# A decoder block's opening re-ordered: scale and norm in one VectorE step, shift added where the halves are split

## The chip, the cores and the metric

The kernel runs on one core of a Trainium2 chip. The metric is the device time of one execution in microseconds (us), the median of several. Five engines run their own instruction queues in order: TensorE (PE in the profile, with its weight loads as PEld), VectorE (DVE), ScalarE (ACT), GpSimd (POOL) and SyncE (SP, which here only issues transfers).

## The reference

One decoder block over 2048 tokens of width 1024, in float32. What matters here is its head:

```python
c_act = jax.nn.silu(c)
ada = (c_act @ w_ada[l] + b_ada[l])[:, None, :]
shift, scale, gate = jnp.split(ada, 3, axis=-1)
h = _rms(x, g_pre[l]) * (1.0 + scale) + shift     # _rms: x * rsqrt(mean(x*x)+eps) * g
proj = h @ w_in[l]                                # 1024 x 4864
q, k, v, z_a, u_b, v_b, z_b, g_logits = jnp.split(proj, SPLIT_IDX, axis=-1)
q = _rope(...); k = _rope(...)                    # cos and sin of positions * inv_freq
```

Sliding-window attention, a spatial gating unit, two gated projections and an output projection follow; the change leaves them alone.

## The kernel before, in words

**Products.** Every large matrix product is split 2 x 2 and made of seven products of sums of quarters (Winograd's form), numbered p = 0 to 6. Each quarter is split into a high part in the fp32r format and the low rest, and a product of two quarters is three TensorE passes over four tiles of 128 rows: 12 matmuls of 128x512 (`mm3`, lines 158 to 164). One product is a *slot*. A slot needs a weight pair W (high by a ScalarE cast, line 207; low by a VectorE subtraction through line 146) and an activation tile T of four row tiles (high by ScalarE, line 614; low by VectorE, line 146).

**Order.** Nothing is scheduled by a planner: each engine runs its instructions in the order in which the program emits them. `w_get` (195) is called before every slot and lets `want` (181) prepare the weights three slots ahead: fetch (SP), weight sums `s13`, `s2`, `s4` (234 to 262), cast, low part. `later(n, f)` hangs work on the slot n ahead, before its matmuls, after them ("post"), or between their halves ("mid").

**The first 1024 tokens** are the opening. Three column blocks of `w_in` share the activation tiles: slots 0 to 20 are p = 0 for blocks 0, 1 and 2, then p = 1 for them, and so on; their accumulators are banks X and W, Y and Z, and the tile s. The 1024 tokens come as two halves h of 512, x transposed in eight row tiles `xh[kt][h]`. p = 0 needs half 0 and rows 0 to 511; p = 1 needs the difference of the halves, so half 1's statistics; p = 2 and later need rows 512 to 1023 as well, so the second half of scale and shift.

**Ahead of slot 0**, in program order: transfers of half 0, of the first half of w_ada (4 MB), of three weight quarters, of half 1. Ten dummy products `warm` (418). Squares of half 0 (528: ScalarE squares, VectorE adds). `rstd` (538: sums over partitions on TensorE, a VectorE copy, two GpSimd steps) and `rstd_out` (548: spread over the partitions by TensorE, copied by ScalarE). `ada_row` (560): the product c @ w_ada, 32 matmul instructions for each half. `xn` (555): x times the norm, on VectorE, eight tiles. `ada_rows_out`, `ada_fin` (570 to 589): that row turned to columns; VectorE makes the scale A and the shift SH. The rope table (452 to 517) is a chain of 26 VectorE steps on 128x512, handed out by `rope_do(n)` wherever the program calls it; positions come by four GpSimd-issued transfers that repeat each row 32 times. Then `t_part(0, i)` (619) makes T[0]: `h_raw` (591: ScalarE, x*A + SH), high part, low part.

**After slot 2**: `rstd(1)` between the halves of slot 2, `second_half` (1141): two rows of the second ada product, `rstd_out(1)`, `xn` of half 1, T[1], the rest of the ada rows. By then `want` has been asked for slots 3 to 5, so that the sums `s13`, `s2` of blocks 0 to 2 stand ahead of half 1's statistics on VectorE. The last xn stand behind slot 3, T[2] in slot 4, T[3] to T[6] three slots ahead of their use. `cur["cap"]` is the highest weight fetch allowed at a time.

## Time and profile before

| | |
|---|---|
| median of 3 runs | 1236.36 us (1235.69 to 1236.84) |
| the profiled execution | 1237.23 us, of which the span of the trace 1235.5 us |
| mean granted TensorE clock | 0.993 |
| TensorE busy | 1202.1 us, 97% (5494 instructions) |
| VectorE busy | 831.2 us, 67% |
| ScalarE busy | 620.2 us, 50% |
| GpSimd busy | 269.9 us, 22% |
| moved by DMA | 294.41 MB, 238 GB/s |

Busy shares are of the span. A row of instructions gives the start, the busy time, the engine (SPq and the like are the queues that issue transfers), the line, what is written from what, and in brackets the idle time before it and what ended that.

### The profile page before, as it was taken

Reading aid. Unit: us, or ns where it says so; the run is one execution under the profiler, and the core shown is the slowest. Engines: PE = TensorE matmul, PEld = TensorE weight load, DVE = VectorE, ACT = ScalarE, POOL = GpSimd, SP = SyncE. Lnnn points to the kernel's source line nnn. Section 1 sums busy time; section 2 is a strip of 40 time slices with the busy share of each in tenths; the row PEclk is TensorE's granted clock in tenths of the full one; section 3 lists DMA queues with packets and bytes.
Section 4 is the critical chain, followed back from the end, with each engine's and each line's share of the span. In section 5 each row is a group of like instructions: output and inputs, shape, how many; then the busy total and the mean of one; then the engine's idle time right before and its main releaser. Section 6 shows DMA issues by size and latency. Waiting matters only on the chain. (4 is left out here: it accounts for less than half of the span.)

```text
span 1235.5 us, 17177 instructions
## 1 busy us (share of the span) xinstructions
PE 1202.1 (97%) x5494; PEld 959.3 (78%) x5494; DVE 831.2 (67%) x1288; ACT 620.2 (50%) x1340; POOL 269.9 (22%) x247
## 2 busy tenths in 40 slices
PE   7788999999999999999999999999999999999997
PEld 3466887878777777888888787777788888888886
DVE  6787789567767666348766675465756556777775
ACT  3587445476766677434345675455722112444443
POOL 1001556223456200013300001221000000135442
PEclk9899999999999999999999999999999999999999
DMA  9623998766999987478796666988787777854552
GB/s 346 256 77 127 311 334 295 243 185 212 298 341 339 297 298 266 147 225 293 254 281 185 176 183 187 345 252 261 262 295 230 227 247 241 265 179 143 164 179 85
DMA packets 215626, 294.41 MB, mean 238 GB/s; under 512 B 19888, under 2 KB 96304, under 8 KB 215536
## 3 DMA queue, kind: packets, MB, share of 16 engines
q1 hardware_dynamic: 215088, 292.39, 72.7%
q8 instruction: 43, 0.70, 0.2%
q0 software_dynamic: 304, 0.79, 0.2%
q14 instruction: 47, 0.39, 0.1%
q10 hardware_dynamic: 144, 0.13, 0.0%
HBM read 189.75 MB, written 98.24 MB: 233 GB/s over the span
## 5 line engine op out<-in xcount | busy, mean ns | idle before, releaser
L163 PE MATMUL bankY<-T,W 128*128 128x512 f32 x1608 | 390.6, 392 | 1.8 <-ACT bankZ L404 1.0
L163 PEld LDWEIGHTS bankY<-T,W 128*128 128x128 f32 x1608 | 299.4, 188 | 65.3 <-ACT bankZ L404 1.5
L146 DVE TENSOR_TENSOR W<-raw,W 128x512 fp32r<-128x512 f32 x323 | 239.9, 749 | 73.9 <-ACT W L207 73.9
L163 PE MATMUL bankX<-T,W 128*128 128x512 f32 x1140 | 281.0, 395 | 7.4 <-ACT T L614 4.9
L207 ACT CAST W<-raw 128x512 fp32r<-128x512 f32 x323 | 199.4, 618 | 154.7 <-PE b L163 58.0
L163 PEld LDWEIGHTS bankX<-T,W 128*128 128x128 f32 x1140 | 212.5, 189 | 53.4 <-ACT T L614 5.4
L163 PE MATMUL bankW<-T,W 128*128 128x512 f32 x708 | 175.8, 395 | 3.3 <-DVE T L146 2.6
L163 PE MATMUL bankZ<-T,W 128*128 128x512 f32 x708 | 171.1, 390 | 0.0
L163 PEld LDWEIGHTS bankW<-T,W 128*128 128x128 f32 x708 | 131.1, 189 | 35.1 <-DVE T L146 5.7
L163 PEld LDWEIGHTS bankZ<-T,W 128*128 128x128 f32 x708 | 132.2, 188 | 27.3
L149 POOL TENSOR_TENSOR S<-raw,raw 128x512 f32<-128x512 f32 x22 | 29.5, 1341 | 265.2 <-DMA raw<-m 200.3
L149 POOL TENSOR_TENSOR raw<-raw,raw 128x512 f32<-128x512 f32 x44 | 67.0, 1524 | 90.0 <-issue 39.2
L146 DVE TENSOR_TENSOR T<-x,T 128x512 fp32r<-128x512 f32 (+1 forms) x101 | 69.2, 723 | 14.3 <-ACT T L359 8.6
L152 DVE TENSOR_TENSOR e<-bankY,e 128x512 f32<-128x512 f32 x41 | 28.3, 690 | 65.8 <-PE bankY L163 65.2
L163 PE MATMUL s<-T,W 128*128 128x512 f32 x276 | 67.0, 390 | 1.6 <-DVE W L146 1.6
L149 POOL TENSOR_TENSOR S<-x,x 128x512 f32<-128x512 f32 x18 | 25.2, 1408 | 187.9 <-DMA x<-in_wO 178.5
L149 POOL TENSOR_TENSOR raw<-S,raw 128x512 f32<-128x512 f32 x22 | 32.7, 1488 | 139.9 <-DVE W L146 115.3
L163 PEld LDWEIGHTS s<-T,W 128*128 128x128 f32 x276 | 51.6, 188 | 12.7 <-DVE W L146 2.0
L359 ACT CAST T<-x 128x512 fp32r<-128x512 f32 x88 | 49.0, 618 | 4.3 <-PE s L163 4.2
L383 ACT COPY e<-bankW 128x512 f32<-128x512 f32 x41 | 24.0, 584 | 53.6 <-PE bankW L163 51.1
L404 ACT COPY bankZ<-bankY 128x512 f32<-128x512 f32 x42 | 24.0, 570 | 52.4 <-PE bankY L163 52.3
L936 ACT ACTIVATE P<-P,rc 128x128 f32<-128x128 f32 x128 | 44.5, 396 | 11.3 <-DVE rc L932 11.1
(226 smaller groups left out, 1403.2 us busy)
## 6 DMA issues: line engine op xcount, KB each, us to landing
raw<-in_wI SPq DMA_DIRECT2D x128, 256.0 KB, 4.4
raw<-sS SPq DMA_DIRECT2D x84, 256.0 KB, 4.3
g<-e SPq DMA_DIRECT2D x64, 256.0 KB, 3.8
sS<-raw SPq DMA_DIRECT2D x48, 256.0 KB, 4.0
T<-in_wada SPq DMA_DIRECT2D x16, 512.0 KB, 8.2
q<-q SPq DMA_DIRECT2D x64, 128.0 KB, 4.8
q<-k_s SPq DMA_DIRECT2D x64, 128.0 KB, 4.3
raw<-in_wP SPq DMA_DIRECT2D x32, 256.0 KB, 3.8
```

The source lines that it names most:

```text
L146: dve.tensor_tensor(out=o, in0=a, in1=b, op=ALU.subtract)
L149: pool.tensor_tensor(out=o, in0=a, in1=b, op=op)
L152: dve.tensor_tensor(out=o, in0=a, in1=b, op=ALU.add)
L163: pe.matmul(o, w[:, i, sl], t[:, j, kt, :], start=start and kt == kts[0] and n == 0, stop=stop and kt == last and n == 2, skip_group_check ...
L207: act.copy(w[:, 0, :], src)
L359: act.copy(T[p][:, 0, kt, :], rs[kt])
L383: act.copy(self.wsb, b["W"])
L404: act.copy(self.b[to], self.b[of])
L936: act.activation(out=st["P", kv][:, g, 0:P], in_=st["P", kv][:, g, 0:P], func=AF.Copy, scale=st["rc", kv][:, g : g + 1])
```

## The change

- The SP transfer of `col` and the positions go out by ScalarE's queue. Positions come as 4 rows once; `positions()` converts them on VectorE and one TensorE product spreads them over 128 partitions into bank Y, from which the first rope step reads. The rope chain has 25 steps.
- `xn` and `h_raw` go. `scaled` makes x*A*norm in one VectorE step, in `t_part`; for rows 0 to 511 of half 1 the norm is read in bank W. The shift is added in the high part (ScalarE, Identity with a bias) and in the low part (VectorE); T[1] and T[6] are differences in which it falls out, T[4] takes the difference DS.
- Ahead of slot 0: 2 warm products, positions, 6 rope steps, squares of half 0, 8 warm products, the rest as before with 10 rope steps behind the spread norm and two weight pairs. Half 1's squares stand behind `ada_fin(0)`, between the parts of T[0], their adds behind all of T[0].
- `want` prepares only three weights until slot 3; `rstd(1)` stands behind slot 2, the weight sums of block 0 behind half 1's statistics, those of blocks 1 and 2 behind T[1]. The other ada rows stand behind T[1]. Nine rope steps are left for slots 5 to 13.
- Two small transfers move from ahead of slot 0 to slot 3; weight fetches are capped until slot 4.

```diff
-    sp.dma_start(col, colc)
+    act.dma_start(col, colc)
...
     def want(n):
         while cur["prep"] < min(n + 1, len(preps)):
             k = cur["prep"]
             fetch_to(k + 4)
             low_now()
+            sum_to(k + 1)
             ready.append(w_of(preps[k]()))
-            while cur["sum"] < min(k + 2, len(sums)):
-                for f in sums[cur["sum"]]:
-                    f()
-                cur["sum"] += 1
+            sum_to(k + 1 + cur["ahead"])
             fetch_to(k + 5)
             cur["prep"] += 1
...
-        want(n + LA)
+        want(min(n + LA, max(2 * n - 2, NFIRST - 1)))
...
-    for g in range(NG):
-        pool.dma_start(posi[32 * g : 32 * (g + 1), :], pos[g : g + 1, :].broadcast_to([32, TG]))
+    posi = ropew[0:NG, 7, :].bitcast(I32)
+    act.dma_start(posi, pos)
...
-        dve.tensor_copy(a, posi)
-        yield
-        tsc(a, a, col[:, C_INV : C_INV + 1], ALU.mult)
+        tsc(a, BK["Y"], col[:, C_INV : C_INV + 1], ALU.mult)
...
-    def xn(kt, h):
-        dve.tensor_tensor(out=xh[kt][h], in0=xh[kt][h], in1=rbs[h], op=ALU.mult)
+    def positions():
+        f, pick = ropew[0:NG, 5, :], ropew[0:NG, 4, 0:P]
+        dve.tensor_copy(f, posi)
+        dve.tensor_copy(pick.rearrange("p (g r) -> p g r", g=NG), ident[0:NG, 0:NG, None].broadcast_to([NG, NG, 32]))
+        pe.matmul(BK["Y"], pick, f, start=True, stop=True,
+                  skip_group_check=True)
+
+    def scaled(kt, h):
+        dve.scalar_tensor_tensor(out=xh[kt][h], in0=xh[kt][h], scalar=A[:, kt : kt + 1],
+                                 in1=BK["W"] if h == 1 and kt < 4 else rbs[h], op0=ALU.mult, op1=ALU.mult)
...
     def t_hi(p, kt):
-        act.copy(T[p][:, 0, kt, :], t_src(p, kt))
+        sh = t_shift(p, kt)
+        if sh is None:
+            act.copy(T[p][:, 0, kt, :], t_src(p, kt))
+        else:
+            act.activation(out=T[p][:, 0, kt, :], in_=t_src(p, kt), func=AF.Identity, bias=sh)
...
     def t_lo(p, kt):
+            dve.scalar_tensor_tensor(out=T[p][:, 1, kt, :], in0=t_src(p, kt), scalar=sh,
+                                     in1=T[p][:, 0, kt, :].bitcast(F32), op0=ALU.add, op1=ALU.subtract)
...
     T[0], T[1] = t_new(), t_new()
+    warm(2)
+    positions()
+    rope_do(6)
     squares(0, range(KT))
-    warm(10)
+    warm(8)
     ada_row(0, range(0, 1))
     rstd(0, BK["Z"])
-    rope_do(7)
     ada_row(0, range(1, 2))
     rstd_out(0, BK["W"])
+    rope_do(10)
     ada_row(0, range(2, 8))
-    for kt in range(KT):
-        xn(kt, 0)
-    want(0)
+    want(1)
     low_now()
-    rope_do(7)
-    squares(1, range(2))
     ada_load(1)
-    cur["cap"] = 1 << 30
-    sp.dma_start(mcpt, mcp)
-    sp.dma_start(snk8, sinks.broadcast_to([P, 8]))
+    cur["cap"] = 10
     ada_rows_out(0)
-    warm(2)
+    warm(1, 2)
     ada_fin(0)
-    squares(1, range(2, 4))
+    warm(3)
+    squares(1, range(0, 2), False)
     for i in range(6):
         t_part(0, i)
-    want(NFIRST - 1)
-    squares(1, range(4, KT))
+        if i == 2:
+            want(NFIRST - 1)
+        elif i == 4:
+            low_now()
+        squares(1, range(i + 2, i + 3), False)
+    square_sums(1)
...
                 def second_half():
+                    rstd(1, BK["Z"])
                     ada_row(1, range(2))
                     rstd_out(1, BK["W"])
-                    for kt in range(4):
-                        xn(kt, 1)
+                    sum_to(NFIRST + 1)
+                    want(NFIRST)
                     for i in range(6):
                         t_part(1, i)
+                        if i == 2:
+                            low_now()
                     ada_row(1, range(2, 8))
                     ada_rows_out(1)
-                later(2, lambda: rstd(1, BK["Z"]), "mid")
+                    cur["ahead"] = 1
...
                 for n in range(5, 15):
-                    later(n, lambda n=n: rope_do(1 if n < 14 else 26))
+                    later(n, lambda n=n: rope_do(1 if n < 14 else 26), True)
```

## Rows read from the trace of the kernel before

**Rows 1.** The table of stages: for stretches of the span (us from its start) the length, then each engine's busy us with its instructions, the granted TensorE clock, DMA share and GB/s. The bounds are starts of TensorE's products: slot 0 at 32.22, the second ada rows at 45.65, slot 3 at 58.40, slot 7 at 73.16, 10 at 82.88, 13 at 93.19, 16 at 104.33, 19 at 114.81.

```profile
32.22:45.65 13.43, 11.80 (x45) 8.69 (x45) 10.43 (x16) 7.18 (x13) 0.00 (x0) 0.84 0.81 313
45.65:58.40 12.75, 9.75 (x42) 4.05 (x41) 8.40 (x15) 4.67 (x8) 1.21 (x2) 0.87 0.70 247
58.40:73.16 14.76, 12.90 (x58) 9.78 (x57) 12.66 (x25) 11.93 (x21) 0.00 (x0) 1.00 0.01 2
73.16:82.88 9.72, 8.73 (x37) 6.60 (x36) 8.17 (x15) 8.55 (x14) 0.00 (x0) 1.00 0.12 34
82.88:93.19 10.31, 9.06 (x37) 6.53 (x36) 9.10 (x16) 7.36 (x13) 0.00 (x0) 1.00 0.59 197
93.19:104.33 11.14, 9.02 (x37) 6.60 (x36) 7.89 (x14) 10.08 (x15) 0.95 (x1) 1.00 0.30 95
104.33:114.81 10.48, 9.41 (x41) 6.91 (x40) 10.11 (x16) 6.85 (x11) 2.16 (x2) 1.00 0.45 152
...
150.00:200.00 50.00, 50.00 (x233) 41.35 (x233) 43.36 (x58) 24.92 (x50) 30.13 (x28) 1.00 0.93 322
```

**Rows 2.** TensorE's instructions in order of time, up to slot 9.

```profile
1.11 11.20 PE L420 MATMUL bankX<-ones 128*128 128x512 f32 x20 [1.11 <-DVE nhalf L126]
13.43 1.08 PE L566 MATMUL b<-T,cact 128*64 128x512 f32 x4 [1.12 <-DMA T<-in_wada]
14.44 1.05 PE L541 MATMUL bankZ<-ones,e 128*128 128x2 f32 x8
...
18.75 5.37 PE L566 MATMUL b<-T,cact 128*64 128x512 f32 x24
...
26.89 1.05 PE L578 MATMUL b<-cst,e 128*128 128x2 f32 x8 [0.85 <-ACT e L572]
32.22 5.20 PE L163 MATMUL bankX<-T,W 128*128 128x512 f32 x12 [4.27 <-ACT T L614]
37.26 2.90 PE L163 MATMUL bankY<-T,W 128*128 128x512 f32 x12
...
42.24 1.20 PE L163 MATMUL s<-T,W 128*128 128x512 f32 x4 [1.63 <-DVE W L146]
...
50.58 2.08 PE L550 MATMUL bankW<-cst,rs 128*128 128x128 f32 x8 [3.00 <-POOL rs L143]
...
75.91 2.88 PE L163 MATMUL s<-T,W 128*128 128x512 f32 x12
78.63 1.75 PE L163 MATMUL bankX<-T,W 128*128 128x512 f32 x7
```

**Rows 3.** The weight loads of the warm products, one early and one late; busy time and the idle time before it together are the distance from one pass to the next.

```profile
5.54 0.34 PEld L420 LDWEIGHTS bankX<-ones 128*128 128x128 f32 x1 [0.52 <-issue]
...
11.29 0.19 PEld L420 LDWEIGHTS bankX<-ones 128*128 128x128 f32 x1 [0.24 <-issue]
```

**Rows 4.** VectorE's instructions in order of time: the last add of half 0's squares, a rope step, the scale (L588), a train of low parts, the adds that stand ahead of slot 2's low part and half 1's ss copy.

```profile
9.15 4.67 DVE L152 TENSOR_TENSOR e<-e,m 128x512 f32<-128x512 f32 x6 [0.36 <-ACT m L535]
...
16.17 0.48 DVE L457 TENSOR_SCALAR T<-T,col 128x512 f32<-128x512 f32 x1
...
18.79 0.43 DVE L457 TENSOR_SCALAR T<-T 128x512 f32<-128x512 f32 x1
...
29.94 0.16 DVE L588 SCALAR_TENSOR_TENSOR AS<-AS,col 128x4 f32<-128x4 f32 x1
...
34.64 0.69 DVE L146 TENSOR_TENSOR T<-wT,T 128x512 fp32r<-128x512 f32 x1 [0.53 <-ACT T L614]
35.25 0.68 DVE L146 TENSOR_TENSOR T<-Tt,T 128x512 fp32r<-128x512 f32 x1
...
38.51 3.07 DVE L152 TENSOR_TENSOR e<-e,m 128x512 f32<-128x512 f32 x4
...
48.99 0.15 DVE L544 COPY ss<-bankZ 128x4 f32<-128x4 f32 x1
```

**Rows 5.** ScalarE's instructions in order of time: the first, the copy of the ada rows, which stands behind two squares of half 1, h_raw and the high part, a change of function table.

```profile
3.00 0.21 ACT L414 ACTIVATE ss<-col 128x8 f32<-128x8 f32 x1 [0.49 <-DMA col<-in_colc]
...
26.27 0.57 ACT L572 COPY e<-b 128x512 f32<-128x512 f32 x1
...
33.29 0.81 ACT L593 ACTIVATE Tt<-Tt,AS 128x512 f32<-128x512 f32 x1
34.01 0.60 ACT L614 CAST T<-wT 128x512 fp32r<-128x512 f32 x1
...
101.78 1.28 ACT L516 ACT_TABLE_LOAD   x1
```

**Rows 6.** Transfers issued in the first 60 us: issuing queue, count, size of each, median us from issue to landing.

```profile
T<-in_pos POOLq DMA_DIRECT2D x4, 64.0 KB, 5.6
...
col<-in_colc SPq DMA_DIRECT2D x1, 21.0 KB, 2.2
```

**Rows 7.** GpSimd's two steps of the norm, for half 0 (15.79) and for half 1 (49.23).

```profile
15.79 0.40 POOL L142 TENSOR_SCALAR pw<-ss 128x4 f32<-128x4 f32 x1 [12.23 <-DVE ss L544]
16.27 1.34 POOL L143 TENSOR_TENSOR rs<-pw,nhalf 128x4 f32<-128x4 f32 x1
49.23 0.19 POOL L142 TENSOR_SCALAR pw<-ss 128x4 f32<-128x4 f32 x1 [31.62 <-DVE ss L544]
49.51 1.02 POOL L143 TENSOR_TENSOR rs<-pw,nhalf 128x4 f32<-128x4 f32 x1
```

More of the change, by code (lines that the diff above doesn't have):

```diff
@@ L133, in hybrid_block @@
     A, SH = AS[:, 0:KT], AS[:, KT : 2 * KT]
+    DS = const([P, 16], "DS")[:, 0:4]
     wT = const([P, 4, P], "wT")
@@ L167, in hybrid_block @@
     loads, preps, sums, ready = [], [], [], []
-    cur = {"load": 0, "prep": 0, "sum": 0, "cap": 3}
+    cur = {"load": 0, "prep": 0, "sum": 0, "cap": 2, "ahead": 0}
     taken, due = [0], []
@@ L179, in fetch_to, with sum_to @@
             cur["load"] += 1
+    def sum_to(n):
+        while cur["sum"] < min(n, len(sums)):
+            for f in sums[cur["sum"]]:
+                f()
+            cur["sum"] += 1
     def want(n):
@@ L416, in hybrid_block, with warm @@
     dve.tensor_scalar(out=cact, in0=cact, scalar1=0.5, scalar2=None, op0=ALU.mult)
-    def warm(n):
+    def warm(n, m=4):
         for _ in range(n):
-            pe.matmul(BK["X"], ones, wide, start=True, stop=True, skip_group_check=True)
+            pe.matmul(BK["X"][:, 0 : m * P], ones, wide[:, 0:m, :], start=True, stop=True, skip_group_check=True)
     adaw = [[T_new(F32).rearrange("p (a b) -> p a b", a=4) for _ in range(2)] for _ in range(2)]
@@ L526, in hybrid_block, with squares @@
     sq, rbs, rs0 = [None, None], [None, None], [None, None]
-    def squares(h, kts):
+    sq_of = []
+    def squares(h, kts, now=True):
         for kt in kts:
@@ L533, in squares, with square_sums @@
             else:
-                t = flat("m")
+                t = flat("m") if now or kt < 5 else flat("e")
                 act.activation(out=t, in_=xh[kt][h], func=AF.Square)
-                add(sq[h], sq[h], t)
+                sq_of.append(t)
+                if now:
+                    square_sums(h)
+    def square_sums(h):
+        while sq_of:
+            add(sq[h], sq[h], sq_of.pop(0))
     def rstd(h, b):
@@ L584, in tt @@
             dve.tensor_tensor(out=dst, in0=a, in1=b, op=op)
-        tt(SH[:, c4], o2[:, 0], col[:, C_BSH + 4 * hf : C_BSH + 4 * hf + 4], ALU.add)
         tt(A[:, c4], o2[:, 1], col[:, C_BSC + 4 * hf : C_BSC + 4 * hf + 4], ALU.add)
@@ L589, in ada_fin @@
                                  op0=ALU.add, op1=ALU.mult)
-    def h_raw(kt, h):
-        c1 = slice(kt, kt + 1)
-        act.activation(out=xh[kt][h], in_=xh[kt][h], func=AF.Identity, scale=A[:, c1], bias=SH[:, c1])
+        tt(SH[:, c4], o2[:, 0], col[:, C_BSH + 4 * hf : C_BSH + 4 * hf + 4], ALU.add)
+        if hf:
+            tt(DS, SH[:, 4:8], SH[:, 0:4], ALU.subtract)
     T = [None] * 7
@@ L602, in t_y, with t_shift @@
         if p < 4:
-            h_raw(kt + 4 * (p > 1), (0, 1, 1, 0)[p])
+            scaled(kt + 4 * (p > 1), (0, 1, 1, 0)[p])
+    def t_shift(p, kt):
+        if p in (1, 6):
+            return None
+        return DS[:, kt : kt + 1] if p == 4 else SH[:, kt + 4 * (p > 0) : kt + 4 * (p > 0) + 1]
     def t_d(p, kt):
@@ L613, in t_hi @@
             T[p] = t_new()
[L614 to L617 removed]
+        sh = t_shift(p, kt)
[3 more added lines that the diff above has]
+            act.activation(out=T[p][:, 0, kt, :], in_=t_src(p, kt), func=AF.Identity, bias=sh)
+    def t_lo(p, kt):
+        sh = t_shift(p, kt)
+        if sh is None:
+            sub(T[p][:, 1, kt, :], t_src(p, kt), T[p][:, 0, kt, :].bitcast(F32))
+        else:
+            dve.scalar_tensor_tensor(out=T[p][:, 1, kt, :], in0=t_src(p, kt), scalar=sh,
+                                     in1=T[p][:, 0, kt, :].bitcast(F32), op0=ALU.add, op1=ALU.subtract)
     def t_part(p, i):
@@ L1141, in second_half, with fetch_all @@
                 def second_half():
+                    rstd(1, BK["Z"])
                     ada_row(1, range(2))
                     rstd_out(1, BK["W"])
-                    for kt in range(4):
-                        xn(kt, 1)
+                    sum_to(NFIRST + 1)
+                    want(NFIRST)
                     for i in range(6):
                         t_part(1, i)
+                        if i == 2:
+                            low_now()
                     ada_row(1, range(2, 8))
                     ada_rows_out(1)
-                later(2, lambda: rstd(1, BK["Z"]), "mid")
+                    cur["ahead"] = 1
+                def fetch_all():
+                    cur["cap"] = 1 << 30
                 later(2, second_half, True)
+                later(4, fetch_all, True)
                 later(3, lambda: ada_fin(1), "mid")
-                for kt in range(4):
-                    later(3, lambda kt=kt: xn(4 + kt, 1), True)
-                later(4, lambda: dve.tensor_scalar(out=snk8, in0=snk8, scalar1=1.0 / SM, scalar2=None, op0=ALU.mult))
+                later(3, lambda: sp.dma_start(mcpt, mcp))
+                later(3, lambda: sp.dma_start(snk8, sinks.broadcast_to([P, 8])))
+                later(9, lambda: dve.tensor_scalar(out=snk8, in0=snk8, scalar1=1.0 / SM, scalar2=None, op0=ALU.mult))
                 for i in range(6):
```

2 lines of the change are left out of this document (removed).

## The prediction

> **What bounds the kernel now.** I read the engine shares first: TensorE is busy 97% of the span, so a change elsewhere counts only where TensorE waits. The table of stages shows where [rows 1]. From 150 to 200 us TensorE is busy 50.00 of 50.00 us; up to 114.81 every stage is longer than TensorE's work in it. A slot of 12 matmuls takes 2.72 to 2.73 us where nothing stalls (start of slot 8 to start of slot 9, 75.91 to 78.63 [rows 2]). Three slots are 8.2 us, and the stages of three slots last 9.72, 10.31, 11.14 and 10.48 us [rows 1]. So some 8.5 us are lost between 73.16 and 114.81, more between 32.22 and 73.16, and the whole time to slot 0, 32.22 us, holds no product of the block. The change touches only this opening. What it gains by slot 19 it keeps, if the later stages still run without gaps.
>
> The opening is a relay. Half 0's squares (their last add ends at 13.82 [rows 4]) free the norm at 14.44, the ada rows end at 24.12, the columns of A start at 26.89 [rows 2], A is there at 30.10 [rows 4], slot 0 starts at 32.22. Then half 1's statistics and the rest of the ada rows fill 45.65 to 58.40, with TensorE busy 9.75 of 12.75 us [rows 1].
>
> **The head, up to A.** The positions' transfer now stands on ScalarE behind the tanh, which ends at 3.21 [rows 5]; with an issue of 0.4 us it leaves at about 3.6. Small transfers landed after 2.2 us (col) and 5.6 us (the old positions) [rows 6]; this one is small but meets the same traffic as the latter. I take 3.0, so 6.6, with 5.8 to 9.2 as bounds. A cast (0.43, as a rope step of one input [rows 4]) and a small copy give 7.3. The spreading product is two passes of 0.43 or 0.86 us (busy plus idle in the weight loads [rows 3]): 9.1 at the slow rate. Six rope steps ran from 16.17 to 19.22 in the old place, 3.05 us [rows 4]: 12.1. Seven adds at the train's distance of 0.61 us (34.64 to 35.25 [rows 4]) and the last one's end make 4.4: half 0's sum is ready at 16.5, against 13.82. The squares themselves are hidden, since x lands earlier without the repeated positions, but the adds now stand behind the rope.
>
> TensorE: eight warm products are 16 passes, 6.9 us at the fast rate and 13.8 at the slow one. In the kernel before the passes were still slow at 5.54 us, though the ten products stood without a gap from 1.11. Now two products end near 4.5 and TensorE idles until about 7.3, so it may be slow longer. If it is fast at once the warm products end near 14.8; if only some 5 us after 7.3, near 17.7. I take 16.1. One ada row (1.08 [rows 2]) follows, so the norm's sums start at 17.1, which is 2.7 later than 14.44. From there to the end of the ada rows the order is as before, 24.12 - 14.44 = 9.7: 26.8.
>
> What goes is the wait behind it. The old copy of the rows stood behind half 1's first squares until 26.27 [rows 5], and A behind VectorE's rope steps and adds until 30.10. Now the copy (0.57 [rows 5]), the columns (1.05 [rows 2]), two small VectorE steps (0.16 each [rows 4]) and the hand-overs make 2.1: A at 28.9. **Gain 1.2**, with bounds -1.7 (positions at 9.2 or a slow clock) and +2.6.
>
> **Slots 0 to 2.** From A to the end of slot 0's matmuls took 7.16 us (30.10 to 37.26). Now VectorE makes x*A*norm in 0.69 and the low part in 0.69; ScalarE makes the high part with a bias. Its price lies between 0.60 (cast) and 0.81 (scale and bias) [rows 5]; I take 0.71, one operand more than the cast. The four squares between the high parts bring the last high part to A + 5.9, its low part to A + 6.7, and TensorE is through at A + 7.2: no gain, though three warm products keep its clock up (slot 0 ran at 5.20 us for 12 matmuls [rows 2]). The removed h_raw (16 times 0.81 at most) is worth ScalarE time, not this chain. What gains is slot 2: its low weight part stood behind half 1's adds (38.51 to 41.58 [rows 4]) and TensorE waited 1.63 us [rows 2]; the norm's sums stood inside it, for about another 1.3 in all. Now the low part comes between T[0]'s and the sums follow: X end + 2 x 2.73 = A + 12.6 = 41.5, against 45.65. Of these 4.1 us, **2.9** are new.
>
> **Slots 3 to 6.** Before: 45.65 to 73.16, 27.5 us. Now from e = 41.5, norm's sums 0.95, ss and GpSimd 1.55 (48.99 to 50.53 [rows 4, 7]), spreading 1.2: e + 3.8. VectorE, with 13 steps of 0.61 for T[1] and one low part, is through at e + 12.0; the six weight sums of blocks 1 and 2, which stood ahead of the statistics, now follow (3.7: e + 15.7), A's second half 0.5, slot 4's low weight part e + 16.8, T[2] twelve steps to e + 24.8, slot 6's low part e + 25.4, ten matmuls more to e + 27.9. So the statistics go ahead, the ada rows no longer hold slot 3, and slot 4 and slot 6 stall instead by some 3 us each behind VectorE: **-0.4**.
>
> One resource is hit by the move. GpSimd's two steps took 0.19 and 1.02 us with VectorE idle, 0.40 and 1.34 with VectorE in rope steps [rows 7]. Half 1's will now run beside weight sums: **-0.5** by these rows. The Trainium skill ("SBUF — State Buffer", "SBUF: two separate sides") says that VectorE steps with two SBUF inputs and GpSimd steps lock each other out for a whole instruction. By that rule each of the two steps could wait out one VectorE step, -1.4 us in place of -0.5 and a sum of 5.4, an estimate; the rows above show a smaller delay, beside steps of mostly one input.
>
> **Slots 7 to 18**, 73.16 to 114.81, lost 8.5 us. p = 3: T[3] no longer runs through ScalarE twice (0.81 + 0.60 a tile); VectorE gets 14 steps of 0.61 = 8.5 for 8.2 us of slots, just in time: +1.4 of the 1.5 lost. p = 4: 17 steps, 10.4 us, and a pair of table loads (1.28 each [rows 5]) moves here with the first sine: +0.2. p = 5: before, three table loads lay before slot 15's high parts (10.08 us of ScalarE work in 11.14 [rows 1]); now the sines come in slots 10 and 13: +1.5. p = 6 as before. **+3.1.** The bias in 20 high parts costs 20 x 0.10 = 2.0 us of ScalarE, hidden by the 16 h_raw that go; without that cover it would be 2.0.
>
> **Sum.** 1.2 + 2.9 - 0.4 - 0.5 + 3.1 = 6.3. The profiled execution took 1237.23, which gives 1230.9; it lies 0.87 above the median of 1236.36, so the forecast is 1230.1. About 0.2% (2.5 us) is what a measurement can tell from no change.
>
> **Rivals.**
> 1. *The head comes late.* Positions at 9.2 rather than 6.6, or the clock slow until 12: A at 31 to 31.8, the gain 6.3 - 2.5 = 3.8 or less: about 1233. For it: a GpSimd-issued transfer of 64 KB needed 5.6 us in the same traffic [rows 6], and TensorE idles between its two warm groups. Against: the new transfer is 8 KB and the repeated rows that slowed the others are gone.
> 2. *Given back.* The later stages find work due earlier than transfers bring it, DMA being 0.93 busy from 150 to 200 [rows 1]: the time stays 1236. Against: TensorE waits for nothing there.
> 3. *VectorE becomes the bound: slower.* Sixteen scalings are no longer done early, while TensorE is at the ada rows; eight of them (half 0's) stand behind A, 4.9 us, and the six sums behind T[1] are 3.7 us. If nothing hides these and the 3.1 doesn't come, 1.2 + 2.9 - 8.6 = -4.5: 1241. It decides from the point where VectorE has no idle time left in 58.40 to 114.81; it had 56.41 - 47.93 = 8.5 us there [rows 1], mostly waits for ScalarE's high parts, which the change shortens. That speaks against it.
>
> **Chances.** Forecast 0.58 (1226.5 to 1232.5 by itself), late head 0.20, given back 0.14, slower 0.08. Most of the late head still counts as faster: faster 0.75, within 0.2% 0.17, slower 0.08. Low end: A's bound +2.6 in place of +1.2, and VectorE's stalls in slots 4 and 6 half as long, 1230.1 - 1.4 - 2.7 = 1226.0. High end 1236.5 takes in the late head and the unchanged time.
>
> **What would show it.** Right: half 0's norm sums near 17, A near 29, slot 3 starting 9 to 10 us behind slot 2's end, VectorE without gaps from there to slot 9, slot 15 with less wait, TensorE without a gap from about 108.5. Wrong: A later than 31, slots 9 to 18 with longer waits on VectorE's low parts than before, or new waits on transfers after 115.

## The result, and the profile after

The changed kernel takes 1241.15 us (median of 6 runs, 1238.44 to 1242.96), the kernel before on the same chip 1236.52 (6 runs): a ratio of 1.0039, interval 1.0024 to 1.0054. A second set of 8 runs (*after_again*) gave 1240.6 and 1.0034 (1.0021 to 1.0046). The change makes the kernel about 4 us **slower**; 1230.1 was predicted. The profiled execution took 1238.44, with a span of 1236.7, TensorE 1206.4 us busy (98%, x5500) and a granted clock of 0.992. Its whole-kernel figures hardly show a difference; only the stages do. Each runs from one milestone to the next, and a plus is time gained (A is ready when VectorE has made the scale; the slots are as before):

| stage | before, us | after, us | gain | predicted |
|---|---|---|---|---|
| start to A ready | 30.10 | 32.09 | -1.99 | +1.2 |
| A to end of slot 2's products | 15.55 | 12.47 | +3.08 | +2.9 |
| end of slot 2 to slot 7 | 27.51 | 32.13 | -4.62 | -0.9 |
| slots 7 to 9 | 9.72 | 8.18 | +1.54 | +1.4 |
| slots 10 to 12 | 10.31 | 11.44 | -1.13 | +0.2 |
| slots 13 to 15 | 11.14 | 10.99 | +0.15 | +1.5 |
| slots 16 to 18 | 10.48 | 10.93 | -0.45 | 0 |
| sum, to slot 19 | 114.81 | 118.23 | -3.42 | +6.3 |

The two profiled executions end only 1.2 us apart: behind slot 19 the changed kernel's took 1118.5 us and that of before 1120.7. The change doesn't reach there, and the last section shows where most of these 2.2 us lie.

TensorE's instructions of the changed kernel in order of time, with the same columns as [rows 2]:

```profile
1.11 3.51 PE L425 MATMUL bankX<-ones 128*128 128x512 f32 x4 [1.11 <-DVE nhalf L126]
7.99 2.07 PE L570 MATMUL bankY<-T 4*128 4x512 f32 x2 [3.38 <-DVE T L569]
9.99 9.33 PE L425 MATMUL bankX<-ones 128*128 128x512 f32 x16
...
20.26 1.05 PE L551 MATMUL bankZ<-ones,e 128*128 128x2 f32 x8
...
24.59 5.37 PE L585 MATMUL b<-T,cact 128*64 128x512 f32 x24
...
63.45 2.55 PE L164 MATMUL bankZ<-T,W 128*128 128x512 f32 x10 [0.91 <-DVE W L147]
...
72.92 3.93 PE L164 MATMUL bankW<-T,W 128*128 128x512 f32 x10 [3.74 <-DVE W L147]
76.69 2.91 PE L164 MATMUL bankZ<-T,W 128*128 128x512 f32 x12
...
94.95 0.50 PE L164 MATMUL bankW<-T,W 128*128 128x512 f32 x1 [1.29 <-ACT T L640]
...
96.31 4.49 PE L164 MATMUL bankZ<-T,W 128*128 128x512 f32 x12
```

The head first. Between the two warm groups TensorE waits 3.38 us for the positions, and the eight warm products behind the spreading product (two passes each, so x16 in the row) take 9.33 us; the norm's sums, at 14.44 in [rows 2], start at 20.26. Further down, ten products of slot 6 come after 3.74 us behind VectorE and take 3.93 us, and slot 13 takes 4.49 us where slot 7 takes 2.91. The reason for the long products is the clock. Busy time of each engine and the granted clock in short stretches, columns as in [rows 1]:

```profile
6.00:8.00 2.00, 0.01 (x1) 0.01 (x1) 0.55 (x2) 1.69 (x3) 0.00 (x0) 0.91 1.03 376
8.00:10.00 2.00, 2.00 (x3) 0.50 (x3) 0.00 (x0) 0.20 (x1) 0.00 (x0) 0.50 1.06 385
10.00:12.00 2.00, 2.00 (x4) 0.97 (x4) 1.79 (x4) 0.00 (x0) 0.00 (x0) 0.50 1.02 414
12.00:14.00 2.00, 2.00 (x4) 0.88 (x3) 1.93 (x4) 0.00 (x0) 0.00 (x0) 0.50 1.02 414
14.00:16.00 2.00, 2.00 (x5) 0.78 (x4) 1.69 (x4) 1.61 (x3) 0.00 (x0) 0.89 1.03 414
...
60.00:62.00 2.00, 2.00 (x6) 1.59 (x5) 1.93 (x4) 0.11 (x1) 0.00 (x0) 0.50 0.09 10
72.00:74.00 2.00, 1.08 (x3) 0.89 (x4) 2.00 (x5) 1.97 (x4) 0.00 (x0) 0.62 0.10 36
74.00:76.00 2.00, 2.00 (x7) 1.57 (x6) 2.00 (x4) 0.84 (x2) 0.00 (x0) 0.53 0.00 0
96.00:98.00 2.00, 2.00 (x7) 1.55 (x7) 2.00 (x5) 1.97 (x3) 0.00 (x0) 0.59 1.09 374
```

After TensorE's idle time the clock stands at 0.50 (1.2 GHz) until 14; it falls again around the waits in slots 3, 6 and 12. VectorE's instructions of the same kernel show the other half of the head, and what fills the time up to slot 6; below them stand GpSimd's two steps of half 1's norm:

```profile
7.39 0.42 DVE L568 CAST T<-T 4x512 f32<-4x512 int32 x1 [2.94 <-DMA T<-in_pos]
...
13.34 5.46 DVE L153 TENSOR_TENSOR e<-e,m 128x512 f32<-128x512 f32 x7
...
31.93 0.16 DVE L606 SCALAR_TENSOR_TENSOR AS<-AS,col 128x4 f32<-128x4 f32 x1
...
49.84 1.41 DVE L574 SCALAR_TENSOR_TENSOR q<-q,AS,bankW 128x512 f32<-128x512 f32 x2 [2.07 <-ACT e L563]
...
58.07 0.68 DVE L153 TENSOR_TENSOR S<-raw,P 128x512 f32<-128x512 f32 x1
...
64.25 1.41 DVE L574 SCALAR_TENSOR_TENSOR x<-x,AS,e 128x512 f32<-128x512 f32 x2
...
72.18 1.29 DVE L147 TENSOR_TENSOR W<-raw,W 128x512 fp32r<-128x512 f32 x2
...
45.80 0.57 POOL L143 TENSOR_SCALAR pw<-ss 128x4 f32<-128x4 f32 x1 [22.35 <-DVE ss L554]
46.45 1.47 POOL L144 TENSOR_TENSOR rs<-pw,nhalf 128x4 f32<-128x4 f32 x1
```

The seven adds of half 0's squares follow the first rope steps and end at 18.80 (before: 13.82 [rows 4]). Each reads the result of the one before, and they start 0.80 us apart: (5.46 - 0.69) / 6. The same adds did so in the kernel before, six in 4.67 us [rows 4]. ScalarE's squares did not hold them up. The sixth square did wait 5.86 us, since the squares use m buffers that only the adds free, but it ended at 14.69, and the add that reads it began at 16.52.

### The profile page after: what moved, and what is told of

Same layout as the page of the kernel before. It is cut to its first block, busy times and chain, and to the rows that moved or that the text cites. A ratio compares the mean times of both kernels' runs of the same rounds, so it can differ in the third digit from the quotient of the medians.

```text
span 1236.7 us, 17163 instructions
## 1 busy us (share of the span) xinstructions
PE 1206.4 (98%) x5500; PEld 960.7 (78%) x5500; DVE 832.9 (67%) x1290; ACT 610.9 (49%) x1324; POOL 271.2 (22%) x243
## 4 chain that ended last, share of the span: by engine, by line
PE 86%; DVE 5%; DMA 4%; ACT 2%; issue 2%; SPq 1%; POOL 1%; DVEq 0%; ACTq 0%; POOLq 0%
PE bankY L164 27%; PE bankX L164 19%; PE bankZ L164 12%; PE bankW L164 12%; PE s L164 4%; PE b L164 4%; PE b L990 2%; PE s L940 1%; DMA T<-in_wada 1%; PE s L941 1%; PE b L879 1%; PE b L975 1%; DVE W L147 1%; DMA T<-in_xt 0%; DVE T L647 0%
## 5 line engine op out<-in xcount | busy, mean ns | idle before, releaser
L147 DVE TENSOR_TENSOR T<-x,T 128x512 fp32r<-128x512 f32 (+1 forms) x93 | 64.5, 736 | 9.6 <-ACT T L364 9.1
```

Source lines behind the costliest of these rows:

```text
L147: dve.tensor_tensor(out=o, in0=a, in1=b, op=ALU.subtract)
```

## The experiments

Times are medians, with the ratio to the kernel before on the same chip. The milestones (start of half 0's norm sums, of slots 0, 3, 7 and 19) are from each kernel's own profile.

| kernel | us | ratio (interval) | norm sums | slot 0 | slot 3 | slot 7 | slot 19 |
|---|---|---|---|---|---|---|---|
| before | 1236.4 to 1236.9 | 1 | 14.44 | 32.22 | 58.40 | 73.16 | 114.81 |
| after | 1241.15 | 1.0039 (1.0024, 1.0054) | 20.26 | 33.82 | 55.12 | 76.69 | 118.23 |
| after_again | 1240.6 | 1.0034 (1.0021, 1.0046) | 19.54 | 33.10 | 54.39 | 76.28 | 119.69 |
| stats_first | 1234.14 | 0.9982 (0.9971, 0.9992) | 12.57 | 28.10 | 49.58 | 69.44 | 111.98 |
| no_gap | 1241.42 | 1.0043 (1.0029, 1.0058) | 18.02 | 32.12 | 53.42 | 75.32 | 118.18 |
| adds_first | 1240.24 (one) | | 20.86 | 34.42 | 55.72 | 77.18 | 118.14 |
| sums_idle | 1240.19 | 1.0037 (1.0024, 1.0051) | 21.13 | 34.69 | 55.99 | 77.01 | 117.66 |
| t2_early | 1238.89 | 1.0020 (1.0010, 1.0029) | 20.75 | 34.30 | 55.62 | 73.29 | 115.99 |
| keep_warm | 1238.68 | 1.0013 (1.0004, 1.0022) | 20.40 | 33.96 | 55.27 | 75.14 | 116.03 |
| sines_late | 1240.63 | 1.0030 (1.0018, 1.0042) | 19.68 | 34.87 | 56.21 | 77.37 | 117.81 |
| sf_warm | 1233.58 | 0.9979 (0.9969, 0.9988) | 13.19 | 28.91 | 50.33 | 70.19 | 112.75 |
| old_middle | 1242.71 | 1.0059 (1.0041, 1.0078) | 13.45 | 29.20 | 64.86 | 78.58 | 122.60 |
| middle_clean | 1235.45 | 0.9996 (0.9988, 1.0005) | 12.70 | 32.23 | 55.62 | 70.61 | 113.50 |
| mc_warm | 1235.57 | 0.9988 (0.9977, 0.9999) | 13.04 | 30.10 | 56.64 | 68.97 | 113.29 |
| all2 | 1234.33 | 0.9985 (0.9974, 0.9997) | 13.66 | 29.37 | 51.89 | 69.37 | 113.31 |
| all2_fill | 1232.65 | 0.9970 (0.9956, 0.9984) | 13.28 | 30.64 | 52.03 | 71.73 | 111.56 |
| all3 | **1230.29** | 0.9957 (0.9942, 0.9971) | 13.76 | 29.52 | 52.71 | 70.20 | 109.42 |
| all3_fill | 1232.58 | 0.9965 (0.9952, 0.9979) | 13.32 | 29.04 | 51.88 | 69.97 | 109.79 |
| all3_cap4 | 1230.77 | 0.9957 (0.9944, 0.9969) | 13.57 | 29.28 | 50.59 | 68.17 | 107.39 |
| all3_warm | 1231.46 | 0.9958 (0.9944, 0.9973) | 12.89 | 28.60 | 52.95 | 69.79 | 109.01 |

**The head.** *stats_first* puts the statistics ahead of the positions; *no_gap* takes only TensorE's wait away, *adds_first* only VectorE's rope steps ahead of the adds.

```diff
 stats_first
-    warm(2)
-    positions()
-    rope_do(6)
     squares(0, range(KT))
-    warm(8)
+    warm(10)
     ada_row(0, range(0, 1))
     rstd(0, BK["Z"])
+    positions()
...
-    rope_do(10)
+    rope_do(16)
 no_gap
-    warm(2)
+    warm(5)
...
-    warm(8)
+    warm(5)
 adds_first
-    rope_do(6)
     squares(0, range(KT))
+    rope_do(6)
```

> Undoes the place of the positions: all ten warm products and half 0's squares first, positions and 16 rope steps behind half 0's norm sums. Theory (the head is late because the spreading product leaves TensorE idle from 4.6 to 8.0 us at the low clock and because the six rope steps stand ahead of the adds): half 0's norm sums start at 13 to 15 instead of 20.3, A is there at 25 to 27 instead of 32.1, and the whole is 5 to 7 us shorter than the changed kernel, so 1234 to 1236. Rival (the transfers of the ada rows set A, the norm is only their company): A moves by less than 2 us and the time stays within 2 us of the changed kernel.

> Moves three of the eight later warm products ahead of the spreading product, so that TensorE has no gap in its first 8 us; VectorE's order is that of the changed kernel. Theory (two costs stand in the head, the clock and the rope steps ahead of the adds, the later of them counts): warm products end near 13 instead of 19.3, but half 0's sum is still ready only at 17 to 19, so the norm sums start at 17.5 to 19, and the gain is 1.5 to 2.5 us. Rival (the clock alone): norm sums at 14 to 15, gain 5 to 6 us.

> The changed kernel with half 0's squares and adds ahead of the six rope steps on VectorE; TensorE's order as in the changed kernel. Theory (two costs stand in the head side by side, and taking away one alone leaves the other): half 0's sum is ready near 12 to 13, but the warm products still end at 18.5 to 19.3 at the low clock, so the norm sums start at 19.5 to 20.5 and A moves by less than 1 us. Rival (the rope steps ahead of the adds are the whole cost): norm sums near 14, A 5 us earlier.

TensorE in *stats_first*:

```profile
1.11 10.32 PE L425 MATMUL bankX<-ones 128*128 128x512 f32 x20 [1.11 <-DVE nhalf L126]
...
12.57 1.05 PE L551 MATMUL bankZ<-ones,e 128*128 128x2 f32 x8
```

And in *no_gap*:

```profile
8.11 1.12 PE L570 MATMUL bankY<-T 4*128 4x512 f32 x2 [0.34 <-DVE T L569]
9.16 4.56 PE L425 MATMUL bankX<-ones 128*128 128x512 f32 x10
...
18.02 1.05 PE L551 MATMUL bankZ<-ones,e 128*128 128x2 f32 x8 [3.29 <-DVE e L153]
```

In *adds_first* the adds on VectorE, then the warm products on TensorE:

```profile
8.26 5.45 DVE L153 TENSOR_TENSOR e<-e,m 128x512 f32<-128x512 f32 x7
...
10.24 9.68 PE L425 MATMUL bankX<-ones 128*128 128x512 f32 x16
```

With the statistics first the norm's sums start at 12.57 and the kernel gains 6.5 us on *after_again* (1240.6 to 1234.14). The two other runs show that two costs lay side by side: without TensorE's gap its warm products are through by 13.7, but the sums wait 3.29 us for the adds; without the rope steps ahead of them the adds end at 13.71, but the warm products still hold the sums until 20.86. The adds take 5.45 us here too, with no square late: their distance is their own. Either mended alone brings at most 2.2 us at the sums, and neither shows in the time.

**Slots 3 to 6.** *sums_idle* brings all nine weight sums into VectorE's idle time around half 1's statistics. *t2_early* adds a low part and the first parts of T[2] behind slot 3.

```diff
 sums_idle
     square_sums(1)
+    sum_to(NFIRST + 1)
...
-                    sum_to(NFIRST + 1)
+                    sum_to(2 * NFIRST)
                     want(NFIRST)
 t2_early (with sums_idle)
+                later(3, low_now, True)
                 for i in range(6):
-                    later(4, lambda i=i: t_part(2, i), i > 2)
+                    later(3 if i < 3 else 4, lambda i=i: t_part(2, i), i < 3)
```

> The head as in the changed kernel; the nine weight sums of blocks 0 to 2 go into VectorE's idle time around half 1's statistics: three behind half 1's adds, six behind the ss copy, none behind T[1]. Theory (slots 4 and 6 stall because six weight sums stand behind T[1] on VectorE): the waits for low weight parts of 0.9 us in slot 4 and 3.7 us in slot 6 go, slot 7 starts 3 to 4 us earlier than 76.7, the time is 3 to 5 us shorter than the changed kernel. Rival (VectorE is the bound over the whole stretch, so the work only moves): slot 7 within 1 us of 76.7 and the later slots as before.

> The weight sums in VectorE's idle time as in the run before, and in addition the first three parts of T[2] behind slot 3 rather than ahead of slot 4, that is ahead of the weight casts that on ScalarE stand behind slot 3's eviction. Theory (slot 6 waits because T[2]'s twelve VectorE steps start only when slot 3's eviction has let two weight casts through; VectorE idled 3.7 us just before): slot 6's wait of 3.4 to 4.2 us falls to under 1.5, slot 7 starts 2.5 to 3.5 us earlier against slot 3's start than in the changed kernel, time 2 to 4 us below the changed kernel. Rival (the steps only change places and slot 4 or 5 waits instead): the start of slot 7 against slot 3 within 1 us of the changed kernel's 21.6.

VectorE in *sums_idle*:

```profile
60.47 0.68 DVE L147 TENSOR_TENSOR W<-S,W 128x512 fp32r<-128x512 f32 x1
63.95 0.69 DVE L147 TENSOR_TENSOR W<-S,W 128x512 fp32r<-128x512 f32 x1 [2.79 <-ACT W L212]
```

and ScalarE in the same run:

```profile
62.19 0.59 ACT L388 COPY m<-bankW 128x512 f32<-128x512 f32 x1 [2.88 <-PE bankW L164]
...
63.29 0.62 ACT L212 CAST W<-S 128x512 fp32r<-128x512 f32 x1
```

*sums_idle* took the sums off VectorE there and gained nothing: VectorE now idled 2.79 us for a weight cast that stands on ScalarE behind the copy of slot 3's bank, which waits for slot 3's products. T[2] behind it started at 64.56 against 64.25. The theory that the sums set slot 6's wait fell. *t2_early* puts work into that idle time: the wait in slot 6 falls to 1.65 us, slots 3 to 6 take 17.7 us (21.6 in the change). But slots 10 to 15 then take 22.8 us against 21.4 in *sums_idle*, at a low clock in slot 13, and of 3.7 us gained at slot 7 against *sums_idle* 1.3 are left in the medians, no more than noise (the intervals of the two ratios overlap).

**The clock.** *keep_warm* adds six dummy products inside the three waits; *sines_late* moves the last nine rope steps from slots 5 to 13 to slots 8 to 14, and with them the two sines and the change of ScalarE's function table that comes with each: the load of the first, at 91.85 in slot 12, now stands at 100.75 in slot 14.

```diff
 keep_warm
+                def fill(n):
+                    b = bank()
+                    for _ in range(n):
+                        pe.matmul(b, ones, wide, start=True, stop=True, skip_group_check=True)
+                later(3, lambda: fill(1), "mid")
+                later(6, lambda: fill(3))
+                later(12, lambda: fill(2), "mid")
 sines_late
-                for n in range(5, 15):
+                for n in range(8, 15):
                     later(n, lambda n=n: rope_do(1 if n < 14 else 26), True)
```

> The changed kernel with six dummy products (512 columns, into an unused bank) where TensorE waits: one ahead of the second half of A in slot 3, three ahead of slot 6, two in the middle of slot 12. Nothing else is altered. Theory (each of these waits lets TensorE's clock fall to its low level, and the matmuls behind it run at half rate, about 4.5 us in all in the first profile): the granted clock stays at its high level from 15 to 120 us, slot 6's last ten matmuls take 2.6 instead of 3.9 us, slot 13 2.9 instead of 4.5 us, and the time is 2 to 4.5 us shorter than the changed kernel's 1240.6, with less spread. Rival (the clock is company of the waits and costs nothing by itself): the dummies fill idle time and the time is that of the changed kernel within 1 us, or longer.

> The changed kernel with its last nine rope steps in slots 8 to 14 rather than 5 to 13, so that the two sines with their table loads come in slots 13 and 14 as in the kernel before. Theory (slot 12's wait for the last high part of T[4], some 3 us with the low clock behind it, is the first sine's table load put in ScalarE's queue ahead of it): slot 12 waits under 1.5 us, but slots 15 and 16 lose what they had gained (the kernel before lost 2.95 us there), so slot 13 starts 2 to 3 us earlier, slot 16 0 to 1 us earlier, time within 1.5 us of the changed kernel. Rival (slot 12 waits for VectorE): slot 12's wait as before the move.

TensorE in *keep_warm*, with the dummies (L1195) in slot 6's wait:

```profile
68.78 2.74 PE L1195 MATMUL b<-ones 128*128 128x512 f32 x6
...
72.74 2.57 PE L164 MATMUL bankW<-T,W 128*128 128x512 f32 x10 [0.76 <-DVE W L147]
...
95.79 2.89 PE L164 MATMUL bankZ<-T,W 128*128 128x512 f32 x12
```

The ten products behind the wait take 2.57 instead of 3.93 us, slot 13 takes 2.89 instead of 4.49, the clock is 1.00 from 20 to 120, and the time falls to 1238.68 from 1240.6: the low clock behind the waits costs about 2 us. Useless work is faster than none here. *sines_late* did its part in place (from slot 10 to 13 9.77 us instead of 11.44) and brought nothing in the time: the sines' cost returned in slots 16 to 18 (12.6 us instead of 10.9).

**The order of the middle.** *old_middle* was to show that the new order behind A costs something by itself, but a weight fetch that came too late covered that. *middle_clean* repeats it with the fetches of before.

```diff
 middle_clean (from stats_first; old_middle: only the lines of second_half, want and ahead)
-    cur = {"load": 0, "prep": 0, "sum": 0, "cap": 2, "ahead": 0}
+    cur = {"load": 0, "prep": 0, "sum": 0, "cap": 3, "ahead": 1}
...
-        want(min(n + LA, max(2 * n - 2, NFIRST - 1)))
+        want(n + LA)
...
-    want(1)
+    want(0)
     low_now()
+    squares(1, range(2))
     ada_load(1)
...
-    squares(1, range(0, 2), False)
+    squares(1, range(2, 4))
     for i in range(6):
         t_part(0, i)
...
+    want(NFIRST - 1)
+    squares(1, range(4, KT))
...
                 def second_half():
-                    rstd(1, BK["Z"])
...
+                later(2, lambda: rstd(1, BK["Z"]), "mid")
```

> The positions behind half 0's norm sums as in the run before, and in addition the middle put back to the order of the kernel before: weights prepared three slots ahead from slot 0 on, so the weight sums stand ahead of half 1's statistics, and half 1's norm sums between the halves of slot 2. Theory (the new order of the middle costs time by itself, since the sums then stand behind T[1]; from the end of slot 2 to the start of slot 7 it took 30 to 32 us against 27.5): the time is 1.5 to 4 us below the run with only the positions moved (2.7 us below the kernel before), so 4 to 7 below the kernel before. Rival (the statistics ahead of the sums are worth having, only what stands behind is badly placed): slot 3 starts 2 to 3 us later and the time is the same or longer than with the positions alone.

> Statistics first, as in stats_first, and behind column A's readiness the order of the kernel before: its fetches (block 0's second and third input ahead of the second half of the modulation matrix), half 1's squares added as they come, the third stationary part behind the parts of T[0], the middle statistics inside slot 2, weights three slots ahead. The new step for norm and scale and the new high and low parts stay. It leaves nothing of the computation out. Theory (the new order of the middle, not the new steps, costs the slots 3 to 6): slot 0 starts at 28 to 29 us as in stats_first, end of slot 2 to slot 7 takes 23 to 25 us as in old_middle (32.1 with the change, 27.5 before), slot 0 to slot 7 under 39 us against 41.3 in stats_first, and the whole 1230 to 1233. Rival (the steps themselves cost it: the scaled step on VectorE in place of ScalarE's): slot 0 to slot 7 stays at 41 us or more, the whole at 1233.5 or above.

TensorE in *old_middle*:

```profile
44.52 3.78 PE L164 MATMUL bankX<-T,W 128*128 128x512 f32 x8 [13.26 <-DVE T L647]
```

and VectorE there, with the reason:

```profile
41.00 0.69 DVE L153 TENSOR_TENSOR S<-raw,P 128x512 f32<-128x512 f32 x1 [10.75 <-DMA P<-in_wI]
```

A weight sum that waits for its transfer stood ahead of T[0]'s low parts. *middle_clean* has no such wait. From the end of slot 2 (45.78) to slot 7 it takes 24.8 us, as the theory said, against 30.5 in *stats_first*; but slot 0 starts at 32.23 instead of 28.10, and the whole is 1.3 us slower. Its profile doesn't compare the orders alone, though: with the same instructions ahead of A the clock fell to 0.50 in the head, and A came at 29.29 instead of 26.5. So one warm product was added where TensorE waits in the head, for both: *sf_warm* is stats_first with it, *mc_warm* middle_clean, and *all3_warm* the kernel all3 of the next part.

```diff
     rstd(0, BK["Z"])
+    warm(1)
     positions()
```

> stats_first with one more warm product of four tiles between half 0's norm sums and the spreading of the positions, where TensorE waited 0.71 us; it computes the same. In stats_first's profile the clock stayed at 1.00 from 12 to 24 there and column A was ready at 26.5; in middle_clean's, with the same instructions ahead of A, it fell to 0.50 from about 15 to 21 and A came at 29.29. If this fall is what spreads the runs, sf_warm holds A at 26.5 to 27 always: median 1233 to 1234, with less spread than stats_first (1232.3 to 1239.0). If not, 1234 to 1235.5.

> middle_clean with the same extra warm product, so that the two orders behind A are compared with the same head; it computes the same. Theory (from A on the order of before is faster to slot 7, by the 1.6 us that the two profiles show: 41.3 against 42.9): A at 26.5 to 27, slot 7 at 68 or earlier, the whole 1231.5 to 1233.5, below sf_warm. Rival (the new order is not slower; slot 0's wait behind half 1's squares takes back what slots 3 to 6 gain): slot 7 at 68.5 or later, the whole no lower than sf_warm's, 1233 to 1235.5.

> all3 with the same extra warm product; it computes the same. all3's rows from half 0's norm sums to the end of the ada rows took 11.8 us against 10.2 in stats_first, at a low clock in between. If the product holds the clock there: slot 0 at about 28 instead of 29.5, the whole 1228.5 to 1230. Rival (the gain is lost again at slots 3 to 6 or in the wait near 790): 1230 to 1231.5.

TensorE in *mc_warm*:

```profile
13.96 1.10 PE L425 MATMUL bankX<-ones 128*128 128x512 f32 x2
14.99 1.12 PE L570 MATMUL bankY<-T 4*128 4x512 f32 x2
...
30.10 0.80 PE L164 MATMUL bankX<-T,W 128*128 128x512 f32 x1 [3.89 <-ACT T L640]
31.33 5.05 PE L164 MATMUL bankX<-T,W 128*128 128x512 f32 x11 [0.44 <-DVE T L647]
...
48.56 1.16 PE L560 MATMUL bankW<-cst,rs 128*128 128x128 f32 x8 [2.98 <-POOL rs L144]
```

The product fills the wait, the clock stays at 1.00 up to A, and A comes at 27.16 (27.31 in *sf_warm*). Now the order of before pays in its own places: half 1's squares and adds stand ahead of the first scaled tile, so slot 0 waits 3.89 us and then runs at a low clock (5.05 us for eleven products), and the spreading waits 2.98 us. At slot 7 it is 1.2 us ahead all the same (68.97 against 70.19), at slot 19 0.5 behind, and in the medians 2.0 us behind (1235.57 against 1233.58; the intervals overlap). No more is shown than that the new order behind A is no loss. But from A to slot 7 the change takes 42.9 us in *sf_warm*, where the kernel before took 43.06: the 2.0 us that the forecast had there (2.9 less 0.9) don't come even with the head mended. *sf_warm* itself lies 0.6 us below *stats_first*, within the noise, and *all3_warm* gains nothing on *all3*, though its slot 0 starts 0.9 us earlier.

**Together.** *all2* is stats_first with sums_idle and t2_early; *all3* adds sines_late. *all2_fill* and *all3_fill* add the dummies of keep_warm, *all3_cap4* changes one number of all3:

```diff
 all3_cap4
-    cur = {"load": 0, "prep": 0, "sum": 0, "cap": 2, "ahead": 0}
+    cur = {"load": 0, "prep": 0, "sum": 0, "cap": 4, "ahead": 0}
```

> Three changes together: positions behind half 0's norm sums, the weight sums in VectorE's idle time, the first half of T[2] behind slot 3. By the sum of the single runs (6.5 us for the first, 1.2 us for the other two, both against the changed kernel) 1.2 + 2.7 = 3.9 us below the kernel before; if the clock stays up more, up to 6. Rival: the parts share one wait and the sum is not more than the first alone, 2.7 below.

> The same three and the last rope steps in slots 8 to 14. In the run with these alone slot 13 came 3.3 us earlier against slot 10 and slot 19 lost half of that again, with no change of the whole time. Theory: 0 to 1.5 us below the run with the three. Rival: no difference, what slot 12 gains slots 15 and 18 give back.

> The three and the six dummy products of the run that kept the clock up (against the changed kernel they were worth 1.4 to 2 us). Theory: the waits of slots 3 and 6 are shorter here, so three dummies ahead of slot 6 (2.2 us) now cost about 1 us of slots that would have run, and the two in slot 12 still save about 1.5: within 1 us of the run with the three. Rival (the clock still falls in slots 3, 6 and 12): 1.5 to 3 us below it.

> all3 with the six dummy products of keep_warm in the waits ahead of slots 3, 6 and 12; it computes the same. If the low clock behind the remaining waits still costs time in all3, as it did in the change (1.9 us there) and in all2 (1.7 us): 1228 to 1229.5. If all3 has no such waits left, the products cost their own 1 to 2 us of TensorE: 1230 to 1232. all3's granted clock was 0.996 over the span, which speaks for the second.

> all3 with block 0's second and third input fetched ahead of the second half of the modulation matrix instead of behind it (one number: the cap on early fetches 4 instead of 2); it computes the same. In all3 VectorE waited 1.82 us for them at 39.3 to 41.1 us, and the statistics of half 1 stood behind it, so that TensorE waited 2.49 us for GpSimd. Theory (that transfer sets the wait): the statistics come 1.5 to 2 us earlier, slot 3 starts at about 50 instead of 52, the whole 1228.5 to 1230. Rival (the second half of the matrix, now later, is what slot 3's ada row waits for, or the loss reappears at slots 4 to 6): 1230 to 1231.5.

*all2* is no faster than stats_first. Its slots 3 to 6 take 17.5 us against 19.9, but at slot 7 the two are level (69.37 and 69.44): the 2.4 us had been lost before slot 3, where the norm's sums come 1.1 us later and half 1's spreading waits 1.80 us for GpSimd instead of 0.66. Slots 7 to 15 then take 33.0 us against 31.6. With the sines out of the way as well, *all3* has three slots in 8.2 us from slot 7 to 10 and slot 13 at 88.13, and takes **1230.29 us**, by its ratio 3.6 to 7.2 us less than the kernel before: the lowest median, level with *all3_cap4* and *all3_warm*. With the dummies all2 comes out 1.7 us lower and all3 2.3 us higher, and both pairs of intervals overlap: a gain from dummies is shown in the changed kernel alone. In all3 the wait in slot 12 is shorter to begin with (0.81 us, against 1.30). *all3_cap4* starts slots 3, 7 and 19 each 2 us earlier, as its theory said, and is not faster: the last section shows where these 2 us went in the profiled executions.

## Why the prediction was wrong

**The head: the failed step.** The forecast put the end of the warm products at 16.1, the norm's sums at 17.1 and A at 28.9; measured were 19.3, 20.26 and 32.09. The spreading product started at 7.99 (7.3 forecast), and right was all that follows the sums: 9.70 us to the end of the ada rows (9.7 forecast) and 2.13 from there to A (2.1). What failed is the stretch between, on two engines at once. The first failed term is TensorE's sixteen passes, which were put at something between the fast and the slow rate: behind the idle 3.38 us the clock was low until 14 and they took 9.33 us. The second is half 0's sum, put at 16.5, which came at 18.80. Its adds were costed at 0.61 us from one to the next, 4.4 in all. That is the distance of two low parts, which don't read each other's result; these adds do, the kernel before has them 0.80 apart [rows 4], and they took 5.46. They also started at 13.34 instead of 12.1, since the spreading product came 0.7 us later, took 2.07 us at the low clock and had the six rope steps behind it. Rival 1 named the late head, up to A at 31.8, and gave it 0.20: A came there, a little past that end. The price, about 1233, was too low, since slots 3 to 6 missed by as much again. "The squares themselves are hidden" was right: none held an add up.

**Slots 0 to 2** were right: 12.47 us from A to the end of slot 2 (12.6 forecast), +3.08 (2.9).

**Slots 3 to 6** were mis-sized: 32.1 us for 28.4 (e + 27.9, and 0.5 for GpSimd), and the sum of the misses is known from VectorE's rows. T[1] was through 13.6 us behind the end of slot 2 (e + 12.0 forecast): the two GpSimd steps took 0.57 + 1.47 beside VectorE's weight sums, 0.83 more than [rows 7] instead of 0.5; VectorE then waited until 49.84, 2.07 us, for the spread norm and its copy. The six sums took 4.2 (3.7), a second low part that the working had left out stood ahead of T[2] with its wait (0.9), T[2] itself took the 8.0 forecast, and the last ten products and their low clock 3.8 (2.5). That the stalls would move to slots 4 and 6 was right; slot 4's was 0.91 us (2.49 in *after_again*) and slot 6's 3.74, each against some 3. *sums_idle* shows that a sum of VectorE's work alone was not enough: with less work VectorE waited for ScalarE, and *sf_warm* that the new order and steps together gain 0.2 us from A to slot 7 instead of 2.0.

On GpSimd, the Trainium skill ("SBUF — State Buffer", "SBUF: two separate sides") lets a VectorE step with two SBUF inputs and a GpSimd step lock each other out for a whole instruction; the prediction's estimate by that rule was -1.4. Measured is -0.83, between it and the rows' -0.5: each of the two steps took about 0.4 us longer (0.57 for 0.19, 1.47 for 1.02), less than one VectorE step of 0.69. A delay of a whole instruction shows elsewhere in the same trace: beside a GpSimd sum of 1.58 us (from 108.96) one VectorE subtraction took 1.79 us (from 109.30), where the same step took 0.69 at 108.11.

**Slots 7 to 18.** p = 3 was right (8.18 us for 8.3). p = 4 was wrong: the pair of table loads was costed, but not where it stands. ScalarE's rows in slot 12:

```profile
91.85 1.28 ACT L510 ACT_TABLE_LOAD   x1
93.14 0.63 ACT L510 ACTIVATE T<-T 128x512 f32<-128x512 f32 x1
93.68 0.60 ACT L212 CAST W<-raw 128x512 fp32r<-128x512 f32 x1
94.19 0.72 ACT L640 ACTIVATE T<-T,DS 128x512 fp32r<-128x512 f32 x1
```

The load, the sine and a cast lie ahead of T[4]'s last high part, TensorE waits 1.29 us for it, and slot 13 runs at the low clock (4.49 us, 1.6 more than slot 7): here a wait costs more than its own length. It needn't: in *sums_idle* and *middle_clean* the same wait (1.30 and 1.29 us) left slot 13 at 2.88. p = 5 gained 0.15 for 1.5, since that slot 13 lies in it; in *sums_idle* its three slots took 9.92 us, a gain of 1.2. So the forecast for p = 5 was near, and whether it came hung on the clock. Slots 16 to 18 lost 0.45; why is not shown. The high part with a bias took 0.72 (0.71 forecast).

**The other rivals.** Rival 2 (given back) has a part: *sines_late* and *all3_cap4* gain in place and not in the time. Rival 3 gave the right time, 1241, for the wrong reason: VectorE did become the limit in slots 3 to 6, at its place, but its price of 8.6 us did not come, and of the 9.7 us between forecast and stages the head alone missed 3.2 and slots 3 to 6 3.7. With the head undone (*stats_first*) the kernel gains 6.5 us, more than the whole loss. That Rival 3 got 0.08 is a fault of the weights: two terms on the chain to A, the clock behind a new gap, which had no row, and the adds behind the rope, which had one that was not used, were let only reduce a gain.

Two slips of the working move nothing: by its own rows slots 7 to 18 had lost 8.9 us (41.65 - 32.76), not 8.5, and the warm products at the fast rate would have ended near 15.1, not 14.8.

## What to carry to other kernels

Before a small job with a late input goes ahead on an in-order engine, write down for each engine what then stands behind it: here one transfer of 8 KB, due at 7.4 us, held TensorE's warm products and VectorE's adds, both ahead of the statistics on which everything waits. Price a train of steps by a row of the same steps, in which each reads the last one's result if these do. Price a new gap on TensorE as the gap and the slower products behind it, and where two delays end at the same point, undo them together before judging either. A wait mended in one place also has to be followed to the end: several of the mends above gained 1 to 4 us at a slot and little in the time. The same new steps with the statistics first and the weight sums, the sines and T[2] spread anew (*all3*) turned a loss of 4 us into a gain of 4 to 7.

## What the hardware showed beyond that

Short waits inside an otherwise busy stretch take the clock down, and not every time. The clearest case lies far behind the change: near 790 us TensorE waits for a read of k. The changed kernel, its first product behind the wait and the twelve products behind the scores:

```profile
790.90 0.35 PE L940 MATMUL s<-q,q 128*128 128x256 f32 x1 [2.48 <-DMA q<-k_s]
...
791.92 2.91 PE L164 MATMUL bankW<-T,W 128*128 128x512 f32 x12
```

The same place in *all3_cap4*:

```profile
779.89 0.36 PE L939 MATMUL s<-q,q 128*128 128x256 f32 x1 [2.38 <-DMA q<-k_s]
...
780.92 4.50 PE L164 MATMUL bankW<-T,W 128*128 128x512 f32 x12
```

After 2.48 us of waiting the twelve products took 2.91 us, with a granted clock of 1.00 from 791 to 796; after 2.38 they took 4.50, with 0.59 from 781 to 783 and 0.56 from 783 to 785. Of 20 profiled kernels 13 had a slower group there (3.55 to 4.50 us, behind waits of 1.90 to 3.79) and 7 had 2.91 (behind waits of 1.87 to 3.11). So the length of the wait alone doesn't decide, and an execution may or may not carry some 1.6 us there. The total follows it: from this read to the end the 7 took 445.8 to 446.5 us, the 13 others 447.5 to 448.7. The profiled execution of before was among the 13 (3.62), that of after among the 7, and 2.1 of the 2.2 us between them behind slot 19 lie from this read on. Over all 20, the stretch from slot 19 to the end took 1118.1 to 1122.6 us, though the kernels hardly differ there: 2 us between two profiled executions prove little. It also explains *all3_cap4*'s profile: of its 2.0 us ahead of *all3* at slot 19 a longer wait (2.38 for 1.92) and the slower group took all, and both kernels start a later product, marked by a wait for VectorE, at 1078.94 and 1078.98. Whether it went so in the runs without a profile is not shown.
